# A one-element factor per softmax map and the sums of a head's norm: from GpSimd to VectorE

## The chip, the cores and the metric

The kernel runs on one core of a Trainium2 chip. A core has five engines, each with a queue of its own that it works through in order: TensorE (PE in the profile; PEld is its loading of weights), VectorE (DVE), ScalarE (ACT), GpSimd (POOL) and SyncE (SP), which here only issues DMAs. They wait for one another through semaphores. The metric is the device time of one execution in microseconds (us), lower being better; stated times are medians of several executions.

## What is computed

One encoder layer is applied to two groups of 1024 tokens with 1024 channels each. After a modulated RMS norm and one combined input projection there are two attention branches: A is grouped-query attention, B is differential attention with 4 heads, each with two 64-wide softmax maps. Both branch outputs are gated, projected, merged and projected once more. The change touches branch B only:

```python
def one(qblk):
    s = jnp.einsum('bqhmd,bkhmd->bhmqk', qblk, k).astype(jnp.float32) * scale
    p = jax.nn.softmax(s, axis=-1)
    pd = (p[:, :, 0] - lam * p[:, :, 1]).astype(v.dtype)
    return jnp.einsum('bhqk,bkhe->bqhe', pd, v)
...
ob = diff_attention(qb, kb, vb, lam)
ob = rms_norm(ob, subln_g) * (1.0 - lam_init)
```

## The kernel before

The two groups run one after the other through the same stages: projections for the first maps ("head"), six attention phases (0 and 1 for branch A, 2 to 5 for the four heads of branch B), and then the merge and output products. In the attention phases three streams of work are woven together: attention units, input projections of later heads (`qkb_gen`, `vb_gen`), and projections for the gates (`z_gen`). A scheduler decides the order on every engine from priorities and from its own estimate of when things are ready, so a small edit of the source can move many rows. A queue is then fixed: an instruction whose inputs aren't ready holds up everything behind it on its engine.

Matmuls work on pairs of halves (a value and its rest), which is why one product takes three matmuls. TensorE is given: 128x256 projections (L569), 128x512 gate projections (L755), scores (L789, L790, four matmuls a unit and map), values (L857 in branch A, L874 in branch B), transposes (L630, L961) and column sums (L885).

**A unit of branch B** covers one head and 256 queries, as two blocks of 128. For each block two softmax maps are made. `softmax_unit` (called in `scores`) issues the scores to PSUM, VectorE takes the negated row maximum (L791) and scales it (L792), ScalarE forms the exponentials and their sum (L793). The exponentials stay unnormalised: with sums su0 and su1, the difference of the two maps is formed as p0 + f·p1, where f = −lambda·su0/su1. So after the second map VectorE takes the reciprocal of su1 (L818), GpSimd multiplies it by su0 and by −lambda (L819), and in `flip` VectorE adds the maps with that factor (L833) and transposes the 32x32 blocks (L834). SyncE's queue then moves the result into place with four DMAs (L843), and TensorE multiplies by the values (L874, 8 matmuls a unit). There are 2 groups, 4 heads, 4 units a head, 2 blocks a unit: 64 factors.

**The norm of a head.** `b_values` squares the result (L878), sums the squares on TensorE (L885) and copies the sums to `ss` (L887). At the last of the four units (pr == 3) the head's norm is prepared: since the maps are unnormalised, the epsilon is weighted with su0 squared: su := su·su (L890), su := su·2·HD·EPS (L891), ss := ss + su (L892), ss := ss^(−1/2) (L893, a power, on GpSimd). These are [128, 8] tiles, 8 heads in all. The result is read only in `gated_gen` (L961), behind the attention phases.

**What else GpSimd does there.** For each 128-token tile of the next head's q and k: the power of its norm (L590), a product with it (L593), gains (L723) and the rotary steps (L615, L618 twice, L619), all on the tile `row`. L590 waits for two VectorE instructions, L588 and L589, which follow ScalarE's L584 and L585. `pairs_T` then has TensorE transpose `row` (L630). GpSimd also makes the low halves of weights (L195, L237). In the branch B phases `by_turns` gives all of the rotary work to GpSimd.

## Time and profile before

| | |
|---|---|
| median of 3 runs | 1890.05 us (1888.87 to 1896.09) |
| the profiled execution's own time | 1885.75 us |
| its span, first to last instruction | 1884.0 us |
| first factor of the first group, last of the second | at 468.7 us, at 1688.7 us |

The span's views speak of the profiled execution, whose own time is 4.30 us below the median of the runs and 1.75 us above its span. Busy time of PE counts overlapping matmuls once. A row of the groups names the line, the engine, the operation, the tile written and the tiles read, the shape and the count; behind the bar stand the busy time, the mean of one in ns, the idle time of the engine just ahead of these instructions, and who ended it. A row of the timeline has the start, the length, and in brackets the idle time ahead of it with its releaser.

### The profile page before, as it was taken

The numbers are of one execution on the slowest core, as the hardware profiler recorded it, in microseconds if no ns is written. First come the engines' busy times: TensorE is split into PE (matmuls) and PEld (weight loads), VectorE is DVE, ScalarE is ACT, GpSimd is POOL, SyncE is SP. The second block draws the span as 40 slices with busy tenths as digits, with TensorE's granted clock in tenths as the row PEclk, the third lists the DMA queues.
The fourth block names the chain that finished last, engine by engine and source line by source line (L and its number), as shares of the span: only waits on it lengthen the run. The fifth ranks groups of instructions, "written<-read, shape, count | busy, mean of one in ns | idle before, by whom it ended". The sixth has DMA issues, their size and how long they took to land.

```text
span 1884.0 us, 29900 instructions
## 1 busy us (share of the span) xinstructions
PE 1837.1 (98%) x10398; PEld 1552.8 (82%) x10398; DVE 1227.3 (65%) x2016; ACT 777.3 (41%) x1544; POOL 610.7 (32%) x888
## 2 busy tenths in 40 slices
PE   6999999999999999999999999999999999999999
PEld 3798878888899877888889887788888898888887
DVE  5777766454776777347466687665357856773795
ACT  4544434343554544213223444344344545442241
POOL 1343311442453452221233333014354635232100
PEclk7999999999999999999999999999999999999999
DMA  9135776564444467754631567666524443675442
GB/s 324 57 94 160 208 197 181 147 181 143 124 113 121 132 205 226 236 154 134 209 134 52 158 180 196 191 183 187 163 72 133 120 117 101 177 245 171 129 129 90
DMA packets 283895, 295.46 MB, mean 157 GB/s; under 512 B 41952, under 2 KB 236640, under 8 KB 283744
## 3 DMA queue, kind: packets, MB, share of 16 engines
q1 hardware_dynamic: 283744, 293.54, 53.1%
q8 instruction: 83, 1.36, 0.3%
q14 instruction: 68, 0.56, 0.1%
HBM read 133.98 MB, written 42.01 MB: 93 GB/s over the span
## 4 chain that ended last, share of the span: by engine, by line
PE 67%; issue 4%; DMA 4%; DVE 3%; POOL 3%; SPq 2%; ACT 1%; ACTq 0%; POOLq 0%; DVEq 0%
PE f L755 16%; PE f L569 14%; PE f L1029 7%; PE a L874 5%; PE s L789 4%; PE s L790 4%; PE a L857 3%; PE s L1029 3%; PE f L1064 3%; PE s L1064 2%; PE f L1136 2%; SPq L843 1%; PE s L1136 1%; DMA q<-p 1%; DMA st<-in_w_in_dram 1%
## 5 line engine op out<-in xcount | busy, mean ns | idle before, releaser
L755 PE MATMUL f<-u,w 128*128 128x512 f32 x2232 | 565.7, 396 | 1.0 <-POOL w L195 0.8
L755 PEld LDWEIGHTS f<-u,w 128*128 128x128 f32 x2232 | 410.5, 189 | 83.8 <-POOL w L195 1.8
L569 PE MATMUL f<-w,u 128*128 128x256 f32 x3456 | 472.7, 287 | 1.8 <-ACT row L584 0.6
L569 PEld LDWEIGHTS f<-w,u 128*128 128x128 f32 x3456 | 449.7, 192 | 23.2 <-issue 3.3
L791 DVE TENSOR_REDUCE m<-s 128x1 f32<-128x1024 f32 x256 | 309.4, 1217 | 104.4 <-PE s L790 102.4
L195 POOL TENSOR_TENSOR w<-st,w 128x512 fp32r<-128x512 f32 x160 | 214.1, 1356 | 394.5 <-ACT w L193 375.6
L834 DVE STREAM_TRANSPOSE p<-p 128x1024 f32<-128x1024 f32 x192 | 237.7, 1242 | 84.3 <-ACT p L793 68.2
L793 ACT ACTIVATE p<-s,m,u 128x1024 f32<-128x1024 f32 x128 | 153.9, 1204 | 164.8 <-issue 71.1
L790 PE MATMUL s<-u,sw 128*128 128x512 f32 x512 | 201.5, 398 | 0.0
L793 ACT ACTIVATE p<-s,m,rsB 128x1024 f32<-128x1024 f32 x128 | 153.8, 1203 | 107.2 <-DVE m L792 88.1
L193 ACT ACTIVATE w<-st 128x512 fp32r<-128x512 f32 x184 | 107.4, 626 | 99.5 <-DMA st<-in_w_in_dram 85.7
L1029 PE MATMUL f<-u,w 128*128 128x512 f32 x552 | 131.1, 392 | 0.0
L874 PE MATMUL a<-q,u 128*128 128x256 f32 x512 | 125.1, 381 | 2.8 <-DMA q<-p 1.9
L857 PE MATMUL a<-q,u 128*64 128x256 f32 x1024 | 117.9, 382 | 5.5 <-DMA q<-p 4.9
L1029 PEld LDWEIGHTS f<-u,w 128*128 128x128 f32 x552 | 103.0, 188 | 21.1
L590 POOL TENSOR_TENSOR rsB<-ss,nhalf 128x4 f32<-128x4 f32 x64 | 65.9, 1031 | 150.9 <-DVE ss L589 132.9
L633 DVE TENSOR_TENSOR u<-f,u 64x256 fp32r<-64x256 f32 (+1 forms) x198 | 81.4, 411 | 48.6 <-ACT u L632 43.3
L763 ACT ACTIVATE ev<-f 128x512 f32<-128x512 f32 x93 | 55.2, 594 | 139.0 <-PE f L755 90.3
L790 PEld LDWEIGHTS s<-u,sw 128*128 128x128 f32 x512 | 96.7, 189 | 16.8 <-issue 0.4
L789 PE MATMUL s<-u 128*128 128x512 f32 x256 | 107.6, 425 | 2.9 <-ACT p L793 2.9
L874 PEld LDWEIGHTS a<-q,u 128*128 128x128 f32 x512 | 94.7, 190 | 17.9 <-issue 3.3
L857 PEld LDWEIGHTS a<-q,u 128*64 128x64 f32 x1024 | 76.3, 137 | 40.0 <-issue 10.3
(221 smaller groups left out, 2181.6 us busy)
## 6 DMA issues: line engine op xcount, KB each, us to landing
q<-p SPq DMA_DIRECT2D x768, 128.0 KB, 2.6
st<-in_w_in_dram SPq DMA_DIRECT2D x132, 256.0 KB, 3.2
zd<-ev SPq DMA_DIRECT2D x96, 256.0 KB, 2.6
sw<-u SPq DMA_DIRECT2D x256, 64.0 KB, 2.0
u<-in_w_ada_dram SPq DMA_DIRECT2D x8, 1024.0 KB, 11.4
oo<-zd SPq DMA_DIRECT2D x64, 128.0 KB, 2.3
od<-oo SPq DMA_DIRECT2D x64, 128.0 KB, 2.4
st<-in_w_in_dram SPq DMA_DIRECT2D x64, 128.0 KB, 2.7
```

Of the source, the lines that this page charges most:

```text
L193: nc.scalar.activation(wh, st, AF.Copy)
L195: e.tensor_tensor(out=wl, in0=st, in1=wh.bitcast(F32), op=ALU.subtract)
L569: ins = nc.tensor.matmul(ps, lt[c][:, sl], w[:, c, wi, :], start=(k == 0), stop=(k == 23))
L755: ins = nc.tensor.matmul(ps, w[:, c, wi, e * P : (e + 1) * P], rt[c], start=(k == 0), stop=(k == 23),)
L789: nc.tensor.matmul(s[:, sl], q, k[:, sl], start=True, stop=False)
L790: nc.tensor.matmul(s[:, sl], sw, k[:, sl], start=False, stop=True)
L791: nc.vector.tensor_reduce(out=m, in_=s, axis=AX.X, op=ALU.max, negate=True)
L793: nc.scalar.activation(pt.rearrange("p (j c a) -> p j c a", j=4, c=8), s.rearrange("p (c a j) -> p j c a", c=8, j=4), AF.Exp, bias=m, scal ...
L834: nc.vector.transpose(pt, pt)
L857: lambda k=k, m=m: nc.tensor.matmul(acc[(LO, HI)[m]], u["v"][:, k], pT[m][:, k], start=(k == 0), stop=(k == 7))
L874: nc.tensor.matmul(acc, u["v"][:, k], pT[:, k], start=(k == 0), stop=(k == 7))
L1029: nc.tensor.matmul(ps, w[:, c, wi, d * P : (d + 1) * P], o[:, oi, :], start=(k == 0), stop=(k == 11))
```

## The change

The 64 factors are made by VectorE right behind the reciprocal. The two products on su become one VectorE instruction, and the addition to ss goes to VectorE too; the power stays on GpSimd. So 64 + 24 instructions leave GpSimd, and 64 + 16 are added to VectorE. The operations and their operands are otherwise the same.

```diff
@@ scores
             f = tiny.tile([P, 1], F32, tag="r", name=nm("r"))
             nc.vector.reciprocal(f, su)
-            nc.gpsimd.tensor_scalar(
+            nc.vector.tensor_scalar(
                 out=f, in0=f, scalar1=u["su"][:, qt : qt + 1], scalar2=nlam, op0=ALU.mult, op1=ALU.mult
             )
@@ b_values
             su = u["su"]
-            nc.gpsimd.tensor_tensor(out=su, in0=su, in1=su, op=ALU.mult)
-            nc.gpsimd.tensor_scalar(out=su, in0=su, scalar1=2.0 * HD * EPS, scalar2=1.0, op0=ALU.mult, op1=ALU.mult)
-            nc.gpsimd.tensor_tensor(out=ss, in0=ss, in1=su, op=ALU.add)
+            nc.vector.scalar_tensor_tensor(out=su, in0=su, scalar=2.0 * HD * EPS, in1=su, op0=ALU.mult, op1=ALU.mult)
+            nc.vector.tensor_tensor(out=ss, in0=ss, in1=su, op=ALU.add)
             nc.gpsimd.tensor_tensor(out=ss, in0=ss, in1=nhalf[:, :NTT], op=ALU.pow)
```

The scheduler rearranges the branch B phases of both groups: no matmul and no DMA is added or dropped, the rows up to the first factor of a group are the same, and from the end of branch B on they are the same again. In between PE's rows move by up to some 90 matmuls. The line of the power is L892 in the changed kernel; lines further down are one lower than before. Three places follow, all in the first group; first numbers in a tile's name count the tiles, and are the same in both kernels.

**First place: GpSimd, the last q and k tile of the fourth head** (`row_1109`; the fourth unit of the third head is near, whose norm is prepared here). Before:

```order
L590 TENSOR_TENSOR rsB_111<-ss_1110_7066,nhalf_97 128x4
L819 TENSOR_SCALAR r_1137_7195<-r_1137_7195,suB_2_119,nlam_116 128x1
L593 TENSOR_TENSOR row_1109_7063<-row_1109_7063,rsB_111 128x128
L890 TENSOR_TENSOR suB_2_119<-suB_2_119 128x8
L723 TENSOR_TENSOR row_1109_7063<-row_1109_7063,gB_114 128x2x48
L615 TENSOR_TENSOR rc_1111_7072<-row_1109_7063,tab_508_3287 128x4x16
L618 TENSOR_TENSOR row_1109_7063<-row_1109_7063,tab_508_3287 128x4x8 x2
L891 TENSOR_SCALAR suB_2_119<-suB_2_119 128x8
L619 TENSOR_TENSOR row_1109_7063<-rc_1111_7072,row_1109_7063 128x4x16
```

and with the change, on the same engine:

```order
L590 TENSOR_TENSOR rsB_111<-ss_1110_7064,nhalf_97 128x4
L593 TENSOR_TENSOR row_1109_7061<-row_1109_7061,rsB_111 128x128
L723 TENSOR_TENSOR row_1109_7061<-row_1109_7061,gB_114 128x2x48
L615 TENSOR_TENSOR rc_1111_7070<-row_1109_7061,tab_508_3287 128x4x16
L618 TENSOR_TENSOR row_1109_7061<-row_1109_7061,tab_508_3287 128x4x8 x2
L619 TENSOR_TENSOR row_1109_7061<-rc_1111_7070,row_1109_7061 128x4x16
```

The factor and the two products on su are gone from between the tile's rows. On PE the transpose of this row (L630) stands behind the same six matmuls in both kernels: four gate projections (L755) and the first two score matmuls of `s_1147`.

**Second place: GpSimd and VectorE, the first q and k tiles of the fourth head** (`row_1023`, `row_1032`, `row_1045`; `s_1057` and `s_1065` are scores of a unit of the third head). GpSimd before:

```order
L590 TENSOR_TENSOR rsB_111<-ss_1024_6542,nhalf_97 128x4
L590 TENSOR_TENSOR rsB_111<-ss_1033_6607,nhalf_97 128x4
L593 TENSOR_TENSOR row_1023_6539<-row_1023_6539,rsB_111 128x128
L590 TENSOR_TENSOR rsB_111<-ss_1046_6676,nhalf_97 128x4
L593 TENSOR_TENSOR row_1032_6604<-row_1032_6604,rsB_111 128x128
L723 TENSOR_TENSOR row_1023_6539<-row_1023_6539,gB_114 128x2x48
L615 TENSOR_TENSOR rc_1025_6548<-row_1023_6539,tab_508_3287 128x4x16
L618 TENSOR_TENSOR row_1023_6539<-row_1023_6539,tab_508_3287 128x4x8 x2
L593 TENSOR_TENSOR row_1045_6673<-row_1045_6673,rsB_111 128x128
L723 TENSOR_TENSOR row_1032_6604<-row_1032_6604,gB_114 128x2x48
L618 TENSOR_TENSOR row_1032_6604<-row_1032_6604,tab_508_3287 128x4x8 x2
L619 TENSOR_TENSOR row_1023_6539<-rc_1025_6548,row_1023_6539 128x4x16
```

GpSimd with the change:

```order
L590 TENSOR_TENSOR rsB_111<-ss_1024_6541,nhalf_97 128x4
L593 TENSOR_TENSOR row_1023_6538<-row_1023_6538,rsB_111 128x128
L723 TENSOR_TENSOR row_1023_6538<-row_1023_6538,gB_114 128x2x48
L615 TENSOR_TENSOR rc_1025_6547<-row_1023_6538,tab_508_3287 128x4x16
L618 TENSOR_TENSOR row_1023_6538<-row_1023_6538,tab_508_3287 128x4x8 x2
L619 TENSOR_TENSOR row_1023_6538<-rc_1025_6547,row_1023_6538 128x4x16
```

VectorE at the same place, before:

```order
L833 SCALAR_TENSOR_TENSOR p_1036_6630<-p_1040_6653,r_1044_6664,p_1036_6630 128x1024
L588 TENSOR_REDUCE ss_1024_6542<-row_1023_6539 128x4
L588 TENSOR_REDUCE ss_1033_6607<-row_1032_6604 128x4
L791 TENSOR_REDUCE m_1056_6728<-s_1057_6729 128x1
L834 STREAM_TRANSPOSE p_1036_6630<-p_1036_6630 128x1024
L589 TENSOR_SCALAR ss_1024_6542<-ss_1024_6542 128x4
L589 TENSOR_SCALAR ss_1033_6607<-ss_1033_6607 128x4
L791 TENSOR_REDUCE m_1064_6779<-s_1065_6780 128x1
```

and with the change:

```order
L833 SCALAR_TENSOR_TENSOR p_1036_6629<-p_1040_6652,r_1044_6663,p_1036_6629 128x1024
L834 STREAM_TRANSPOSE p_1036_6629<-p_1036_6629 128x1024
L791 TENSOR_REDUCE m_1056_6726<-s_1057_6727 128x1
L792 TENSOR_TENSOR m_1056_6726<-m_1056_6726,rsB_111 128x1
L791 TENSOR_REDUCE m_1064_6777<-s_1065_6778 128x1
L792 TENSOR_TENSOR m_1064_6777<-m_1064_6777,rsB_111 128x1
L588 TENSOR_REDUCE ss_1024_6541<-row_1023_6538 128x4
L589 TENSOR_SCALAR ss_1024_6541<-ss_1024_6541 128x4
```

GpSimd no longer mixes three tiles but finishes `row_1023` first, while VectorE now takes the sum of `row_1023` (`ss_1024`) behind the maximum of `s_1065`. On PE there stand, with the change, between the last score matmul of `s_1065` and the transpose of `row_1023`, 23 projection, 4 value and 8 score matmuls.

**Third place: VectorE and PE, the first values of a unit of the third head** (`a_1053`, which reads `q_1016`; its last block is `p_1020`, made from the scores `s_1030`). VectorE before:

```order
L818 RECIPROCAL r_1031_6587<-su_1028_6577 128x1
L879 TENSOR_TENSOR oo_1019_6521<-a_1018_6520,oo_1019_6521 128x4x2x32
L833 SCALAR_TENSOR_TENSOR p_1020_6523<-p_1027_6576,r_1031_6587,p_1020_6523 128x1024
L791 TENSOR_REDUCE m_1037_6631<-s_1038_6632 128x1
L834 STREAM_TRANSPOSE p_1020_6523<-p_1020_6523 128x1024
```

and with the change:

```order
L818 RECIPROCAL r_1031_6586<-su_1028_6576 128x1
L819 TENSOR_SCALAR r_1031_6586<-r_1031_6586,suB_2_119,nlam_116 128x1
L833 SCALAR_TENSOR_TENSOR p_1020_6522<-p_1027_6575,r_1031_6586,p_1020_6522 128x1024
L834 STREAM_TRANSPOSE p_1020_6522<-p_1020_6522 128x1024
```

PE before:

```order
L790 MATMUL s_1065_6780<-u_849_5428,sw_1017_6506 128x512
L569 MATMUL f_1035_6620<-w_1007_6462,u_77_328 128x256
L569 MATMUL f_1035_6620<-w_1007_6462,u_78_329 128x256
L874 MATMUL a_1053_6724<-q_1016_6501,u_939_6008 128x256 x8
L789 MATMUL s_1070_6822<-u_848_5427 128x512
```

and with the change:

```order
L569 MATMUL f_1035_6619<-w_1007_6461,u_70_276 128x256 x2
L874 MATMUL a_1053_6722<-q_1016_6500,u_939_6007 128x256 x2
L789 MATMUL s_1057_6727<-u_848_5427 128x512
L569 MATMUL f_1014_6484<-w_1007_6461,u_77_328 128x256
L569 MATMUL f_1014_6484<-w_1007_6461,u_78_329 128x256
L569 MATMUL f_1014_6484<-w_1007_6461,u_77_328 128x256 x2
```

On VectorE factor, addition and transposition now stand in a row. On PE the first value matmul has moved ahead of two maps' scores: between the last score matmul of `s_1030` and it stood 75 projection, 8 value, 16 score and 2 sum matmuls; now 55, 8, 8 and 2.

## Prediction

> **What bounds the kernel now.** I read the totals first, then the two stretches that the scheduler rearranges, then what TensorE waited for in them.
>
> ```profile
> PE 1837.1 (98%) x10398; PEld 1552.8 (82%) x10398; DVE 1227.3 (65%) x2016; ACT 777.3 (41%) x1544; POOL 610.7 (32%) x888
> ...
> 450.00:740.00 290.00, 285.82 (x1696) 249.34 (x1695) 203.93 (x344) 138.41 (x280) 129.60 (x239) 1.00 0.51 146
> 1385.00:1740.00 355.00, 349.31 (x1934) 304.55 (x1933) 237.14 (x380) 162.09 (x318) 151.32 (x245) 1.00 0.51 147
> ```
>
> The last two rows are the windows' view of branch B in each group (length, then busy time of PE, PEld, DVE, ACT, POOL, then the granted clock). PE is busy for 285.82 of 290 and 349.31 of 355 us, at full clock. Its matmuls stay the same, so if every idle moment of PE vanished from both stretches, the gain would be 4.18 + 5.69 = 9.87 us, 0.52% of 1890.05. VectorE is at 203.93 of 290 us (70%), so it has room. The largest of PE's waits in the same two stretches (total, times, longest):
>
> ```profile
> PE f L630 <- POOL row L619: 3.4, 2, 2.2
> PE a L874 <- DMA q<-p: 0.5, 1, 0.5
> ...
> PE f L630 <- POOL row L619: 1.5, 2, 1.2
> PE a L874 <- DMA q<-p: 1.4, 1, 1.4
> ...
> ```
>
> Only these two kinds have GpSimd's small work anywhere ahead of them: transposes that wait for a row of GpSimd (4.9 us), and values that wait for exponentials brought by DMA (1.9 us).
>
> **The busy time that changes engine.** These groups are what moves, and the nearest rows on VectorE.
>
> ```profile
> L819 POOL TENSOR_SCALAR r<-r,suB,nlam 128x1 f32<-128x1 f32 x64 | 22.8, 357 | 185.5 <-DVE r L818 168.6 <-DMA q<-p 9.1 <-DMA sw<-u 7.7
> L890 POOL TENSOR_TENSOR suB<-suB 128x8 f32<-128x8 f32 x8 | 8.9, 1117 | 0.4
> L891 POOL TENSOR_SCALAR suB<-suB 128x8 f32<-128x8 f32 x8 | 2.4, 303 | 0.7
> L892 POOL TENSOR_TENSOR ssB<-ssB,suB 128x8 f32<-128x8 f32 x8 | 1.6, 203 | 29.3 <-DVE ssB L887 22.3 <-DVE m L792 7.0
> L818 DVE RECIPROCAL r<-su 128x1 f32<-128x1 f32 x64 | 10.3, 160 | 52.4 <-ACT p L793 52.0
> L833 DVE SCALAR_TENSOR_TENSOR p<-p,r,p 128x1024 f32<-128x1024 f32 x64 | 87.8, 1372 | 25.6 <-POOL r L819 22.2 <-DMA sw<-u 1.6 <-DMA q<-p 1.1
> L589 DVE TENSOR_SCALAR ss<-ss 128x4 f32<-128x4 f32 x96 | 20.9, 219 | 1.4
> L792 DVE TENSOR_TENSOR m<-m,rsB 128x1 f32<-128x1 f32 x128 | 28.8, 231 | 1.8
> ```
>
> GpSimd loses 22.8 + 8.9 + 2.4 + 1.6 = 35.7 us of work, and its waiting for 64 reciprocals and 8 sums at the head of its queue. VectorE gains 64 factors and 16 instructions of the norm. The trace shows none of these forms on VectorE. From below, the reciprocal's 160 ns, since a small VectorE instruction of this kind is the cheapest here; from above, the 231 ns of the scaling; nothing lies under zero, as instructions are added to an engine. I take 219 ns, the nearest form (two scalars on few elements): 80 x 0.219 = 17.5 us, between 12.8 and 18.5. Against it stand the 22.2 us in 39 waits for GpSimd's factor ahead of L833 (0.57 us each), which go. So VectorE comes out about even, and the 17.5 us lie beside PE's work: were that cover gone in one stretch, half of it (8.7 us) less half the saved wait (11.1 us) would still be no loss. The factor waits for nothing that the reciprocal ahead of it hasn't waited for. The power on GpSimd now waits for VectorE's addition in place of the copy of the sums: 29.3 us for 8 now, with weight splits queued behind it, for which PE waits in neither list above; I put it at nothing, as that wait existed before.
>
> [...]
>
> **First place: GpSimd's queue under the transpose of `row_1109`.** The timeline shows PE's largest wait in either stretch:
>
> ```profile
> 679.98 1.02 POOL L590 TENSOR_TENSOR rsB<-ss,nhalf 128x4 f32<-128x4 f32 x1
> 680.99 0.34 POOL L819 TENSOR_SCALAR r<-r,suB,nlam 128x1 f32<-128x1 f32 x1
> 681.29 0.40 POOL L593 TENSOR_TENSOR row<-row,rsB 128x128 f32<-128x128 f32 x1
> 681.65 1.19 POOL L890 TENSOR_TENSOR suB<-suB 128x8 f32<-128x8 f32 x1
> 682.80 0.38 POOL L723 TENSOR_TENSOR row<-row,gB 128x96 f32<-128x96 f32 x1
> 683.97 0.20 POOL L891 TENSOR_SCALAR suB<-suB 128x8 f32<-128x8 f32 x1
> 684.25 0.32 POOL L619 TENSOR_TENSOR row<-rc,row 128x64 f32<-128x64 f32 x1
> 684.62 0.44 PE L630 MATMUL f<-ident,row 128*128 128x128 f32 x2 [2.18 <-POOL row L619]
> ```
>
> GpSimd runs without a gap, so each start minus the one before is the price: the factor 681.29 − 680.99 = 0.30, L890 682.80 − 681.65 = 1.15, L891 684.25 − 683.97 = 0.28, together 1.73 us. All three leave, and the rows on PE ahead of the transpose stay. The wait shrinks from 2.18 to 0.45: **−1.7 us** (at best −2.2, at worst 0 if the values behind it wait instead).
>
> **Second place: `row_1023`.**
>
> ```profile
> 638.95 0.42 ACT L585 ACTIVATE row<-row 128x256 f32<-128x256 f32 x1
> 639.72 2.00 POOL L590 TENSOR_TENSOR rsB<-ss,nhalf 128x4 f32<-128x4 f32 x2 [4.39 <-DVE ss L589]
> 640.84 0.41 DVE L588 TENSOR_REDUCE ss<-row 128x4 f32<-128x256 f32 x1
> 641.28 0.17 DVE L589 TENSOR_SCALAR ss<-ss 128x4 f32<-128x4 f32 x1
> 645.53 0.32 POOL L619 TENSOR_TENSOR row<-rc,row 128x64 f32<-128x64 f32 x1
> 645.90 0.33 PE L630 MATMUL f<-ident,row 128*128 128x128 f32 x1 [1.23 <-POOL row L619]
> ```
>
> Mixed with two other tiles, GpSimd took 645.85 − 639.72 = 6.1 us from the first power to the finished row. One tile by itself is L590, L593, L723, L615, L618 twice, L619: with the starts of the first place and no guests, 684.57 − 679.98 − 1.73 = 2.9 us. But its sum now stands behind the maximum of `s_1065`. From that map's last score: a maximum (1.2), its scaling (0.2), L588 (0.41), L589 (0.17), then 2.9, about 4.9 us with nothing else in the way. PE has 23 projection, 4 value and 8 score matmuls to do meanwhile, at the steps of these rows:
>
> ```profile
> 630.33 4.95 PE L569 MATMUL f<-w,u 128*128 128x256 f32 x40
> 638.91 3.69 PE L874 MATMUL a<-q,u 128*128 128x256 f32 x16 [0.47 <-DMA q<-p]
> 635.12 0.40 PE L789 MATMUL s<-u 128*128 128x512 f32 x1
> 635.35 0.40 PE L790 MATMUL s<-u,sw 128*128 128x512 f32 x1
> ```
>
> A projection is (635.12 − 630.33) / 40 = 0.12, a value about 3.69 / 16 = 0.23, a score 0.23: 2.8 + 0.9 + 1.8 = 5.5 us. So the row is ready 0.6 us early; a transposition of 1.23 us in VectorE's way would make it 0.6 late. The wait of 1.23 goes to between 0 and 0.6; I take **−1.0 us** (−1.2 to +0.5).
>
> **Third place: the values `a_1053`, where the new order costs.**
>
> ```profile
> 627.16 0.16 DVE L818 RECIPROCAL r<-su 128x1 f32<-128x1 f32 x1 [0.82 <-ACT p L793]
> 627.80 1.28 DVE L833 SCALAR_TENSOR_TENSOR p<-p,r,p 128x1024 f32<-128x1024 f32 x1
> 629.00 1.22 DVE L791 TENSOR_REDUCE m<-s 128x1 f32<-128x1024 f32 x1
> 630.14 1.23 DVE L834 STREAM_TRANSPOSE p<-p 128x1024 f32<-128x1024 f32 x1
> 632.40 3.39 SPq L843 DMA_DIRECT2D q<-p  x4
> ```
>
> The first value matmul (638.91 in the rows above) waits 0.47 us for these DMAs already. PE now has 20 projections and 8 scores less ahead of it: 2.4 + 1.8 = 4.2 us sooner. VectorE is sooner too: the factor follows the reciprocal (627.80 − 627.16 = 0.64 becomes about 0.16 + 0.22, −0.26), and the maximum between L833 and L834 is gone (630.14 − 629.00 = 1.14): 1.4 us. If the transfers then land as long after L834 as now (8.8 us), the wait becomes 0.47 + 4.2 − 1.4 = 3.3 us; if SyncE also issues them at once (they went out 1.0 us after L834's end, over 3.39 us), up to 2 us less, 1.3. So +0.8 to +2.8; I take **+1.5 us**, nearer the lower end, since the issues are what the order moves too.
>
> **The other waits.** The 1.4 us wait of values in the second group keeps its place within a few matmuls, and loses an average factor's wait: **−0.6 us** (−1.4 to 0). The row in the second group that PE waits 1.2 us for has no factor between its instructions: nothing. The DMAs on SyncE's queue (L843, `sw`, weights) are the same in number and move by a dozen places at most; the cost of that is in the third place's range.
>
> **Sum:** −1.7 − 1.0 + 1.5 − 0.6 = −1.8 us. The profiled execution, 1885.75 us (span 1884.0 and 1.75 around it), would become 1883.95. It lies 4.30 us below the median of the runs; on the runs' scale the forecast is 1890.05 − 1.8 = 1888.2 us, **no change that a measurement of this kernel can tell**, which is about 0.5% (9.5 us).
>
> **The rivals.**
>
> *Slower: PE arrives too early at the values.* The third place's mechanism, at more units. For it: the scheduler lets value matmuls start 2.4 + 1.8 us earlier there, by an estimate of VectorE and DMAs that this trace doesn't follow (8.8 us from L834 to the values). Against it: only one of the units is drawn forward so far. It decides once these waits add up to more than the 3.3 us gained elsewhere, i.e. two such places at 2.8. One in each of 8 heads: 8 x 2.8 − 3.3 = +19 us, 1909; in half of them +8, 1898. Chance 0.13, of which 0.09 lie beyond 0.5%.
>
> *Much faster: PE's busy time hides VectorE's wait.* The 22.2 us ahead of L833 lie on a chain through L834 and the DMAs to the values. If PE's matmuls were stretched by it rather than idle, all would come back: 1867.9 us. For it: PE's 98% is a modelled busy time. Against it: 40 projections in a row run at 0.12 us each with nothing to wait for, and PE waits for values only 1.9 us in both stretches. Chance 0.11. [...]
>
> *The change does nothing for PE.* GpSimd's rows wait for VectorE's sums (the 4.39 us ahead of L590 above), not for the factors, and the 1.7 us come back as a later wait of the values. Then the time is 1890 us within the runs' spread. Chance 0.20.
>
> *The forecast*, gains and one loss as summed, up to 6 us either way: 0.56.
>
> **How the numbers follow.** The range goes down to 1879.0, the limit of 9.87 us below 1890.05 and 1.2 for the spread of the runs (the lowest is 1888.87), and up to 1898, half the heads with a third place. Left out are the faster rival (0.11) and the far part of the slower one (0.08). Faster by over 0.5%: 0.11 and 0.01 of the forecast's edge, 0.12. Slower: 0.09. Within: 0.79.
>
> **What would show it.** Right: L819 as a VectorE group at 0.16 to 0.23 us with L833 no longer waiting for GpSimd; the wait at `row_1109` near 0.45 us; one wait of values of 1.3 to 3.3 us near 632 us; idle time of PE in both stretches within 3 us of 9.87. Wrong: PE's busy time in a stretch falling by more than 3 us with the same matmuls (the faster rival), or three or more waits of values over 1 us (the slower one).

## The result and the profile after

| | kernel before | changed kernel |
|---|---|---|
| median | 1890.16 us (20 runs, 1885.55 to 1896.44) | 1894.82 us (20 runs, 1891.70 to 1901.69) |
| ratio to before | | 1.0024, 95% interval 1.0015 to 1.0034 |
| the profiled execution's own time | 1885.75 us | 1893.75 us |

The change costs 4.7 us (a ratio of 1.0024) where 1.8 us were forecast as a gain. The totals, and the two windows of branch B with the same columns as before:

```profile
PE 1839.2 (97%) x10398; PEld 1552.2 (82%) x10398; DVE 1248.0 (66%) x2096; ACT 777.7 (41%) x1544; POOL 585.0 (31%) x800
```

```profile
450.00:740.00 290.00, 283.93 (x1684) 247.17 (x1683) 211.09 (x375) 137.50 (x278) 121.23 (x201) 1.00 0.51 145
1385.00:1740.00 355.00, 345.44 (x1909) 301.13 (x1908) 242.56 (x414) 159.11 (x316) 132.09 (x198) 1.00 0.49 143
```

The work moved as the diff says: VectorE has 20.7 us more, GpSimd 25.7 us less. (The moved rows alone were 35.7 us on GpSimd and are 22.6 us on VectorE. The other rows of GpSimd together take 10.0 us longer than before, those of VectorE 1.9 us less.) TensorE's busy time in the two windows fell because the windows hold 12 and 25 matmuls fewer; in the whole span it is 1839.2 us, 2.1 us more than before. So TensorE now stands idle for 290 − 283.93 = 6.07 and 355 − 345.44 = 9.56 us: 15.6 in place of 9.87. What it waited for (total, times, longest), the first group's stretch and then the second's:

```profile
PE s L789 <- DVE u L633: 1.4, 2, 1.2
PE f L755 <- DVE ssB L887: 1.3, 1, 1.3
PE f L630 <- POOL row L619: 1.2, 1, 1.2
PE a L874 <- DMA q<-p: 1.0, 1, 1.0
```

```profile
PE f L569 <- DVE u L633: 3.6, 1, 3.6
PE f L630 <- POOL row L619: 1.8, 2, 1.0
PE a L874 <- DMA q<-p: 1.7, 1, 1.7
PE f L569 <- DVE ssB L887: 1.3, 1, 1.3
```

The waits for GpSimd's rows fell in the first group from 3.4 to 1.2 us, and rose in the second from 1.5 to 1.8. A kind of wait is new: for VectorE to read a PSUM bank, L633 (the subtraction behind a transpose) or L887 (the copy of the sums). Before, this kind was 0.2 us in the two stretches together; now the rows of projections (L755, L569) that wait so add up to 1.3 + 3.6 + 1.3 = 6.2 us. The scores' 1.4 us (L789) name the same line but are of another kind: they wait for their operand, the tile `u` that L633 writes (see the first place, below).

The largest, 3.64 us, in the timeline of the changed kernel, VectorE's rows and then TensorE's (left out there are the other seven matmuls of the two score tiles):

```profile
1457.53 0.16 DVE L818 RECIPROCAL r<-su 128x1 f32<-128x1 f32 x1 [2.49 <-ACT p L793]
...
1459.35 0.42 DVE L633 TENSOR_TENSOR u<-f,u 64x256 fp32r<-64x256 f32 x1
1459.80 0.17 DVE L890 SCALAR_TENSOR_TENSOR suB<-suB 128x8 f32<-128x8 f32 x1
1459.89 0.41 DVE L588 TENSOR_REDUCE ss<-row 128x4 f32<-128x256 f32 x1
1460.21 1.22 DVE L791 TENSOR_REDUCE m<-s 128x1 f32<-128x1024 f32 x1
1461.35 0.41 DVE L588 TENSOR_REDUCE ss<-row 128x4 f32<-128x256 f32 x1
1461.67 1.24 DVE L834 STREAM_TRANSPOSE p<-p 128x1024 f32<-128x1024 f32 x1
1462.83 1.19 DVE L791 TENSOR_REDUCE m<-s 128x1 f32<-128x1024 f32 x1
1463.94 0.15 DVE L589 TENSOR_SCALAR ss<-ss 128x4 f32<-128x4 f32 x1
1464.12 0.43 DVE L633 TENSOR_TENSOR u<-f,u 64x256 fp32r<-64x256 f32 x1
```

```profile
1458.43 0.40 PE L789 MATMUL s<-u 128*128 128x512 f32 x1
...
1460.28 0.50 PE L885 MATMUL f<-ones_c,at 128*128 128x1 f32 x4
1460.64 0.42 PE L630 MATMUL f<-ident,row 128*128 128x128 f32 x2
1464.70 0.55 PE L569 MATMUL f<-w,u 128*128 128x256 f32 x1 [3.64 <-DVE u L633]
```

The pool of `f` has three banks (`ps_f`, bufs=3). By the rows, at 1461 us they hold a transpose of which VectorE has read one half (`f_2266`), the sums of L885 (`f_2273`) and a second transpose (`f_2279`), and the next projection needs one. VectorE works without a gap, but seven rows and 4.3 us lie between the two readings of `f_2266`. It had stood idle for 2.49 us just ahead, waiting for an exponential.

The same place in the kernel before, TensorE's rows and then VectorE's two readings of the transpose:

```profile
1456.13 1.35 PE L569 MATMUL f<-w,u 128*128 128x256 f32 x10
...
1458.25 0.50 PE L885 MATMUL f<-ones_c,at 128*128 128x1 f32 x4
1458.61 0.96 PE L569 MATMUL f<-w,u 128*128 128x256 f32 x6
1459.41 0.38 PE L630 MATMUL f<-ident,row 128*128 128x128 f32 x2
1460.10 3.01 PE L569 MATMUL f<-w,u 128*128 128x256 f32 x23 [0.31 <-ACT row L584]
```

```profile
1456.25 0.42 DVE L633 TENSOR_TENSOR u<-f,u 64x256 fp32r<-64x256 f32 x1
1458.50 0.43 DVE L633 TENSOR_TENSOR u<-f,u 64x256 fp32r<-64x256 f32 x1
```

There ten projections stand between the two score tiles and six between the sums and the transpose, and TensorE waits 0.31 us.

### The profile page after: what moved, and what is told of

The parts are those of the page before. It is cut to its first block, busy times and chain, and to the rows that moved or that the text cites. A ratio compares the mean times of both kernels' runs of the same rounds, so it can differ in the third digit from the quotient of the medians.

```text
span 1892.0 us, 29929 instructions
## 1 busy us (share of the span) xinstructions
PE 1839.2 (97%) x10398; PEld 1552.2 (82%) x10398; DVE 1248.0 (66%) x2096; ACT 777.7 (41%) x1544; POOL 585.0 (31%) x800
## 3 DMA queue, kind: packets, MB, share of 16 engines
q8 instruction: 83, 1.36, 0.3%
## 4 chain that ended last, share of the span: by engine, by line
PE 65%; DVE 7%; DMA 5%; issue 3%; SPq 2%; ACT 2%; POOL 2%; DVEq 0%; ACTq 0%; POOLq 0%
PE f L755 18%; PE f L569 14%; PE f L1028 7%; PE a L874 4%; PE a L857 4%; PE s L789 4%; PE s L790 4%; PE s L1028 3%; PE f L1135 2%; DVE m L791 2%; DMA q<-p 1%; DMA st<-in_w_in_dram 1%; ACT p L793 1%; PE s L1135 1%; SPq L843 1%
## 5 line engine op out<-in xcount | busy, mean ns | idle before, releaser
L755 PE MATMUL f<-u,w 128*128 128x512 f32 x2232 | 562.5, 395 | 1.8 <-DVE ssB L887 1.3
L569 PE MATMUL f<-w,u 128*128 128x256 f32 x3456 | 475.0, 287 | 7.2 <-DVE u L633 3.6
L755 PEld LDWEIGHTS f<-u,w 128*128 128x128 f32 x2232 | 409.7, 188 | 84.1 <-DVE ssB L887 1.3
L569 PEld LDWEIGHTS f<-w,u 128*128 128x128 f32 x3456 | 451.3, 192 | 28.8 <-issue 6.9
L791 DVE TENSOR_REDUCE m<-s 128x1 f32<-128x1024 f32 x256 | 309.1, 1217 | 102.1 <-PE s L790 100.5
L195 POOL TENSOR_TENSOR w<-st,w 128x512 fp32r<-128x512 f32 x160 | 218.2, 1382 | 506.0 <-ACT w L193 473.5
L834 DVE STREAM_TRANSPOSE p<-p 128x1024 f32<-128x1024 f32 x192 | 237.7, 1243 | 85.3 <-ACT p L793 66.6
L793 ACT ACTIVATE p<-s,m,u 128x1024 f32<-128x1024 f32 x128 | 153.9, 1204 | 165.8 <-issue 69.8
L793 ACT ACTIVATE p<-s,m,rsB 128x1024 f32<-128x1024 f32 x128 | 153.9, 1204 | 122.3 <-DVE m L792 96.5
L193 ACT ACTIVATE w<-st 128x512 fp32r<-128x512 f32 x184 | 108.0, 626 | 102.3 <-DMA st<-in_w_in_dram 86.2
L874 PE MATMUL a<-q,u 128*128 128x256 f32 x512 | 126.4, 380 | 3.1 <-DMA q<-p 2.7
L590 POOL TENSOR_TENSOR rsB<-ss,nhalf 128x4 f32<-128x4 f32 x64 | 67.0, 1048 | 185.3 <-DVE ss L589 165.3
L789 PE MATMUL s<-u 128*128 128x512 f32 x256 | 107.8, 426 | 3.2 <-ACT p L793 1.6
L633 DVE TENSOR_TENSOR u<-f,u 64x256 fp32r<-64x256 f32 (+1 forms) x198 | 81.4, 412 | 43.5 <-ACT u L632 38.2
L874 PEld LDWEIGHTS a<-q,u 128*128 128x128 f32 x512 | 94.7, 189 | 18.7 <-issue 3.7
```

What stands on the lines that cost most here:

```text
L193: nc.scalar.activation(wh, st, AF.Copy)
L195: e.tensor_tensor(out=wl, in0=st, in1=wh.bitcast(F32), op=ALU.subtract)
L569: ins = nc.tensor.matmul(ps, lt[c][:, sl], w[:, c, wi, :], start=(k == 0), stop=(k == 23))
L755: ins = nc.tensor.matmul(ps, w[:, c, wi, e * P : (e + 1) * P], rt[c], start=(k == 0), stop=(k == 23),)
L789: nc.tensor.matmul(s[:, sl], q, k[:, sl], start=True, stop=False)
L791: nc.vector.tensor_reduce(out=m, in_=s, axis=AX.X, op=ALU.max, negate=True)
```

## Where the 8 us between the two profiles lie

I number TensorE's matmuls in order of start (10398 in each kernel) and compare when the same number starts. The changed kernel's profiled run gains 0.3 us up to number 2800, loses 1.2 to 4400 (first group's branch B), loses 1.6 to 7200, gains 1.5 to 8000, **loses 5.3 from 8000 to 8480**, loses 1.7 to 9600, and nothing beyond: 8.0 us in sum. From 4450 to 7200 the two traces have the same rows, so these 1.6 us are of the run; the run of the kernel before that was profiled was also 4.4 us under its median. The other pieces lie where the orders differ and can be the change's own. By far the largest is the stretch from 8000 to 8480, about 1413 to 1503 us. Its window, before and after (same columns):

```profile
1412.46:1496.54 84.08, 82.07 (x481) 72.42 (x480) 67.21 (x115) 44.13 (x94) 47.60 (x91) 1.00 0.44 120
```

```profile
1413.47:1502.90 89.43, 82.80 (x481) 73.33 (x480) 69.47 (x125) 45.32 (x95) 44.29 (x80) 0.98 0.41 112
```

TensorE's idle time there goes from 2.01 to 6.63 us, and 3.3 us of the rise are at the place above. Its busy time is 0.73 us longer, at a granted clock of 0.98. This stretch is the measure in the experiments.

## The experiments

Two questions: is it the work on VectorE or the order? And what in the order? To keep them apart, a kernel is built twice: once to read off the row order that the scheduler gives, and once with that order written down for every engine, whatever engine the moved instructions are on:

```diff
+    for engine, line in hold(engines, rec["moved"]).items():
+        for a, b in zip(line, line[1:]):
+            tc.add_manual_dep(by_key[b], by_key[a].name, ...)
```

A moved instruction stands directly behind the VectorE instruction that feeds it. Where such work goes back to GpSimd (work_back_order_after, norm_order_none), GpSimd's own order is left to the scheduler; by the traces its other 800 instructions then stand in the held order but for 14 and 12 places. Lines cited from the edited kernels are 1 to 4 higher (L634 is L633, L794 is L793, L819 is the reciprocal's L818, L836 is L833, L877 is L874, L888 is L885, L890 is L887). All results, each ratio against the kernel before on the same chip; length and idle time are those of matmuls 8000 to 8480, read from windows like the two above:

| kernel | order, 1st / 2nd group | work on VectorE | ratio, 95% interval | length, idle (us) |
|---|---|---|---|---|
| changed kernel | after / after | all 80 | 1.0024, 1.0015–1.0034 | 89.43, 6.63 |
| work_moved_order_before | before / before | all 80 | 1.0008, 0.9994–1.0022 | 84.59, 2.40 |
| work_back_order_after | after / after | none | 1.0104, 1.0088–1.0120 | 91.02, 7.66 |
| factor_only | free | 64 | 1.0023, 1.0011–1.0035 | 89.61, 6.60 |
| second_group_after | before / after | all 80 | 1.0035, 1.0018–1.0051 | 90.38, 6.28 |
| second_group_before | after / before | all 80 | 1.0003, 0.9991–1.0016 | 86.16, 2.47 |
| before_again | before / before | none | 1.0012, 0.9997–1.0027 | 84.03, 1.99 |
| norm_only | free | 16 | 0.9984, 0.9974–0.9994 | 84.02, 2.00 |
| norm_order_none | as norm_only | none | 0.9998, 0.9987–1.0008 | 84.03, 2.01 |
| norm_order_all | as norm_only | all 80 | 1.0000, 0.9985–1.0014 | 84.58, 2.47 |
| rate_nudged | free, other rates | none | 0.9999, 0.9988–1.0011 | 84.03, 2.00 |
| mended_after | after, two rows moved | all 80 | 1.0023, 1.0012–1.0034 | 89.52, 5.89 |
| mended_more | after, four rows moved | all 80 | 1.0014, 1.0001–1.0027 | 89.98, 6.54 |
| scores_first | after, scores early | all 80 | 1.0021, 1.0009–1.0034 | 88.64, 6.83 |
| scores_first_mended | both | all 80 | 1.0004, 0.9991–1.0017 | 89.09, 5.59 |
| place_spread | after, the place as before | all 80 | 1.0004, 0.9994–1.0014 | 86.14, 4.22 |

### Work or order

**work_moved_order_before** and **work_back_order_after** swap the two.

> All 80 instructions are on VectorE as in the changed kernel, but every engine keeps the order of the kernel before; each moved instruction stands directly behind the VectorE instruction that feeds it (GpSimd's own order is left to the program). Theory O (the time lost comes from the new order of the instructions, the moved work costs nothing): the profiled run within 1883 to 1888 us, ratio to the kernel before 0.998 to 1.000, no TensorE wait of over 1 us for a PSUM read by VectorE (the subtraction L633, the copy of the sums) in the second group's maps. Theory W (VectorE's 20.7 us more of small instructions push back what stands behind them, wherever they stand): most of the 4.6 us, ratio 1.002 to 1.003, and TensorE idle 13 to 16 us in the two stretches of two-map attention.

> The factor and the preparations are on GpSimd as before, but the other instructions of all engines stand in the order of the changed kernel (GpSimd's own order is left to the program). Theory O: the loss stays, ratio 1.002 to 1.004, with the wait of about 3.6 us for L633 near 1461 us still there. Theory W: the loss goes, ratio 0.999 to 1.001. If the order of after is only good with the quick factor (39 waits for GpSimd of 0.3 to 0.8 us come back on VectorE, 22 us in all), the ratio is over 1.004: then order and work belong together.

With the order of before, the work on VectorE leaves the stretch nearly as it was (2.40 us idle). TensorE is idle for 11.0 us in the two windows, against 9.87 before and the 13 to 16 of theory W. That is nearer theory O, though not sharp: the ratio, 1.0008, and the profiled run, 1889.84 us, both lie above O's ranges, and the ratio's interval reaches from 0.9994 to 1.0022. With the order of after the wait near 1461 us is there even with the factor on GpSimd (3.7 us), so it is not the moved work's. But the third case came too: 1.0104. The order of after costs 15 us more if the factor is on GpSimd: VectorE's merge of the maps (L836) then waits 31.4 us for it, where L833 waited 22.2 us in the kernel before. So order and work belong together, and of these two orders it is only in that of after that the move is worth something. The groups of the reciprocal show how the orders differ, before, work_moved_order_before, after, work_back_order_after (behind the bar the idle time ahead of it, and the part that waited for the exponential):

```profile
L818 DVE RECIPROCAL r<-su 128x1 f32<-128x1 f32 x64 | 10.3, 160 | 52.4 <-ACT p L793 52.0
```

```profile
L819 DVE RECIPROCAL r<-su 128x1 f32<-128x1 f32 x64 | 10.3, 160 | 50.0 <-ACT p L794 49.5
```

```profile
L818 DVE RECIPROCAL r<-su 128x1 f32<-128x1 f32 x64 | 10.4, 162 | 73.2 <-ACT p L793 73.2
```

```profile
L819 DVE RECIPROCAL r<-su 128x1 f32<-128x1 f32 x64 | 10.4, 162 | 69.7 <-ACT p L794 69.6
```

In the order of after VectorE waits 17 to 21 us longer ahead of the reciprocal, whoever makes the factor. The 22.2 us of waits for GpSimd are gone (next rows, L833 of work_moved_order_before and of the changed kernel: 1.5 and 1.8 us idle in place of 25.6), but in the one order nothing comes of it, as TensorE had not been waiting for them, and in the other they are replaced.

```profile
L836 DVE SCALAR_TENSOR_TENSOR p<-p,r,p 128x1024 f32<-128x1024 f32 x64 | 84.6, 1323 | 1.5
```

```profile
L833 DVE SCALAR_TENSOR_TENSOR p<-p,r,p 128x1024 f32<-128x1024 f32 x64 | 85.8, 1340 | 1.8
```

**factor_only** (the first hunk of the change alone) and **norm_only** (the second alone), the scheduler free.

> Only the factor (64 of the 80 instructions, some 17 of the 20.7 us) is on VectorE, the preparations of the norm stay on GpSimd, and the scheduler is free: 836 of TensorE's rows stand otherwise than before, nearly as many as in the changed kernel (845). Theory O: the loss follows the order, which is nearly that of the changed kernel: ratio 1.001 to 1.004, with a wait of over 3 us near 1461 us. Theory W: 17 of 20.7 parts of the loss, ratio 1.001 to 1.003, with its idle time spread over many places.

> Only the preparations of the norm (16 of the 80 instructions, in place of 24 on GpSimd) are on VectorE, the factor stays on GpSimd, the scheduler is free: 188 of TensorE's rows stand otherwise than before, and the place near 1461 us should be as before. Theory P (the loss follows the order of the second group's place): matmuls 8000 to 8480 take 84 to 86 us, ratio 0.999 to 1.001. If the preparations on VectorE were what costs, ratio 1.002 to 1.003.

The factor alone brings the order of after, nearly row for row (the traces show another kind of matmul at 88 of TensorE's 10398 places), its 3.6 us wait and its loss. The preparations alone leave the stretch untouched, and the ratio, 0.9984, is under the 0.999 expected at least: the only one whose interval lies below 1. Is that a gain of the order or of the work?

> The order of norm_only with all the work on GpSimd as in the kernel before (GpSimd's own order is left to the program). If the gain of norm_only is one of the order: ratio 0.9975 to 0.9995. If it is one of the preparations made on VectorE: 0.9995 to 1.001.

> The order of norm_only (the fastest so far, ratio 0.9984) with all 80 instructions on VectorE, the factor's 64 directly behind their reciprocals. If the moved work is worth nothing either way and the order decides: ratio 0.9975 to 0.9995, as norm_only. If the factor on VectorE costs (some 17 us more of small instructions): 1.000 or more. If it gains, since 39 waits of VectorE for GpSimd go: under 0.9975.

It is not the order's: the same order gives 0.9998 with no moved work and 1.0000 with all of it, so the gain that was expected with the order did not come. By the letter of the two expectations the preparations then gain on VectorE and the factor costs as much. But the three intervals overlap, norm_only ran on another chip than the other two, and a kernel measured against itself is off by 0.12% (before_again, below). So 0.16% is not shown to be the work's either. In the two orders that keep the stretch whole, this one and that of before, the moved work as a whole is worth nothing that can be told.

**second_group_after** and **second_group_before** join the two orders between the groups, where they agree.

> All 80 instructions on VectorE; the first group in the order of the kernel before, the second group in the order of the changed kernel (the two orders are alike between, so they can be joined there). So far every run in the order of after lost 5.3 to 5.5 us of TensorE's time (6.9 with the work back on GpSimd) between its matmuls 8000 and 8480 (about 1413 to 1500 us), and the run in the order of before 0.5 us. Theory P (the loss is in that place): it is there again, 5 to 5.5 us, less some 1.3 us gained just ahead of it, so 3 to 4 us more than the moved work in the order of before: ratio 1.0015 to 1.003. Theory S (the loss is spread over all the maps, a little for each moved instruction or each reordered row): half of it, ratio 1.000 to 1.0015.

> The other way round: the first group in the order of the changed kernel, the second group in the order of the kernel before, all 80 instructions on VectorE. Theory P: matmuls 8000 to 8480 take 84 to 85 us as before and not 89.4, and the first group gives within 1.2 us of before: ratio 0.999 to 1.0008. Theory S: half of the loss, ratio 1.001 to 1.002, and as much as in the kernel joined the other way.

Theory P holds: the loss goes with the second group's order (1.0035 against 1.0003, intervals apart), and with 6.28 against 2.47 us idle. The first came out larger than the 1.003 expected at most; the second's 86.16 us are longer than the 85 expected at a granted clock of 0.98 in its window, with TensorE busy for 83.69 in place of 82.07 us.

**before_again** and **rate_nudged** ask how much of this any disturbance would do.

```diff
-    (1.229, 1.265, 0.9, 1.0, 0.85, 1.069),
+    (1.229, 1.265, 0.91, 1.01, 0.86, 1.079),
```

> The kernel before, with its own order written down for every engine: the same instructions in the same rows. A measure of what two profiles of one program differ by, and of whether writing the order down costs anything. Expected: ratio 0.9993 to 1.0007, matmuls 8000 to 8480 within 1 us of 84.1 us; the waits of the first profile that are an accident (and not of the order) differ by 1 to 3 us in single places.

> The kernel before, with nothing moved to VectorE, but four rates by which the second group's two-map attention is woven with other work raised by 0.01 (0.9 to 0.91, 1.0 to 1.01, 0.85 to 0.86, 1.069 to 1.079): 460 of TensorE's rows stand otherwise, about as many as the change moves in one group. Theory R (any such disturbance of the order moves the time by as much as the change did, since the order of before is a picked one): ratio 1.001 to 1.005, with a wait of over 1.5 us in the second group that the kernel before doesn't have. Against it: ratio 0.9993 to 1.0007.

The same program measured against itself gave 1.0012 with an interval up to 1.0027, wider than expected; so differences of 0.1% between kernels of this table mean nothing. Single waits differ too: one of values for a transfer, near 760 us where the rows of the three are the same, is absent in the profile of before, 1.36 us in before_again and 2.24 in rate_nudged. Theory R's loss did not come: 0.9999 with 460 other rows on TensorE. One wait of its kind did, 1.78 us of scores for an exponential at 1686 us (the kernel before waits 1.42 us for a transfer there). The nudge is a limited test, too: TensorE's rows differ in kind only between matmuls 8554 and 9505, so the stretch from 8000 to 8480 has its old pattern here, as it has in norm_only and its two followers. What the table does show is that the pattern goes with the loss: in all eight kernels with TensorE's rows of before in the stretch it is idle for 1.99 to 2.47 us, with none to all of the 80 instructions on VectorE, and in the eight that keep after's run of rows near 1461 us, mended ones included, for 5.59 to 7.66 us.

### What in the order

**mended_after** moves two VectorE rows up at the place of the 3.64 us, in the order of after:

```diff
   L588 ss_2264
+  L633 f_2266, second half
   L791 m_2260
+  L887 f_2273
   L588 ss_2277
   L834 p_2235
   L791 m_2270
   L589 ss_2264
-  L633 f_2266, second half
-  L887 f_2273
```

> The changed kernel in its own order with two VectorE rows moved up at one place, near 1460 us: the second subtraction of tile f_2266 stands three reads of PSUM and row sums earlier (behind the first row sum instead of behind two maxima and a transposition), and the copy of the sums f_2273 directly behind the first maximum. Theory O: the wait of 3.64 us on TensorE goes, 0 to 0.6 us are left of it, and the time falls by 3 to 3.6 us against the changed kernel: ratio to the kernel before 1.0003 to 1.001. Theory W: VectorE is late there by all that stands in its queue, so the wait comes back within the next 10 us, for the next subtraction or the next probabilities: ratio 1.002 to 1.003.

**mended_more** moves two more: L792 of `m_2260` directly behind its L791, and the first L633 of `f_2279` ahead of L834.

> As the first mended kernel, in whose profile the wait of 3.64 us was gone but came back 24 matmuls later as a wait of 3.09 us of the scores for the exponential. Here what that exponential waits for is moved up as well: the small product behind the first maximum stands directly behind it (before: behind a transposition, a second maximum and a subtraction), and the next subtraction of tile f_2279 stands ahead of the transposition, so that ScalarE's queue, which waits for it, comes free. Theory Q (only the order of VectorE's queue is at fault; its work fits): both waits go, matmuls 8000 to 8480 take 85 to 86.5 us and not 89.4, and the ratio is 0.9995 to 1.0012. Theory W (VectorE has too much to do in that stretch): 2.5 us or more of the wait turn up once more within 15 us, ratio 1.0018 to 1.003.

What TensorE waited for from 1450 to 1475 us in mended_after, and in mended_more:

```profile
PE s L790 <- ACT p L794: 3.1, 1, 3.1
```

```profile
PE a L877 <- DMA q<-p: 3.0, 1, 3.0
PE s L790 <- ACT p L794: 0.8, 1, 0.8
```

The wait for the bank is gone both times, and one of 3 us takes its place 24 to 28 matmuls on: first the scores wait for an exponential whose maximum was late, then, with that put right, the values wait for the transposed map that L834 now makes later. Theory W came true as to the waits and the stretch; mended_more's ratio, 1.0014, lies between the ranges of the two theories. But W's reason, that VectorE is too full, was still open, since it idles 2.1 and 2.5 us just ahead. **scores_first** goes for that idle time: the score tiles `s_2237` and `s_2241`, woven into eight value matmuls, come whole ahead of them.

```diff
+  L789, L790 s_2237 and s_2241, 8 matmuls in a row
   L874 a_2233, 8 matmuls
-  (L789, L790 of both woven in between, and four behind)
```

> The changed kernel in its own order but for one place, 10 us ahead of the wait at 1461 us: TensorE computes the two score tiles s_2237 and s_2241 whole ahead of the values a_2233, with which they were interleaved (eight rows moved), VectorE takes their maxima at once and multiplies the output of the values after the merge of the maps, and ScalarE takes the two exponentials ahead of the square of the values. VectorE had stood idle there for 2.09 and 2.49 us, for the values and for the second exponential, with the reads of PSUM queued behind. Theory Q (the place is late because of the order, from TensorE's scores on, and VectorE has time enough): the reciprocal at 1457.5 us comes 2.2 to 3.3 us earlier, the wait of 3.64 us shrinks to under 1.2 us and does not come back, matmuls 8000 to 8480 take 85 to 87 us and not 89.4, ratio 1.000 to 1.0012. Theory W (VectorE has too much in that stretch, whatever its order): a wait of 2.5 us or more within 20 us behind, ratio 1.0018 to 1.003.

> The place of scores_first and the first mended place together (the second subtraction of f_2266 and the copy of f_2273 moved up in VectorE's queue). Theory Q: none of the waits for PSUM reads, exponentials or transfers between matmuls 8273 and 8301 is over 0.6 us, matmuls 8000 to 8480 take 84.5 to 86 us, ratio 0.9995 to 1.001. Theory W: 2.5 us or more still waited there, ratio 1.0018 to 1.003.

The reciprocal comes at 1451.97 us, 5.6 earlier (of which 2.2 were this run's lead at matmul 8000), but VectorE then waits 2.23 us for the next scores, and TensorE still 3.0 us for L633. Both together: 2.8 us for the exponential again. scores_first_mended's ratio, 1.0004, doesn't fit its profile, which has the loss (89.09 us); its interval reaches to 1.0017, and I leave it open.

So none of the four orders tried for VectorE's queue takes the wait away while TensorE's run of rows stays. That run differs most from before: in the order of after two score tiles, the sums and a transpose follow one another in 14 matmuls, 8 + 4 + 2, with nothing between them. In the order of before ten and six projections stand between. **place_spread** puts TensorE's rows so, on top of scores_first, and the rows of VectorE and ScalarE there in the pattern of before:

```diff
   L630 f_2266
   L569 f_2267, 12 matmuls
+  L789, L790 s_2261
+  L569 f_2267, 6 matmuls
-  L569 f_2267, 12 matmuls
-  L789, L790 s_2261
   L789, L790 s_2271
   L885 f_2273
+  L569 f_2267, 6 matmuls
   L630 f_2279
```

> The changed kernel in its own order, but with the whole place near 1461 us laid out as in the kernel before: the scores ahead of the values as in scores_first, and in place of two score tiles, the sums and the transposition in one run of TensorE's rows, eight matmuls of the projection stand between the two score tiles and six between the sums and the transposition; VectorE's and ScalarE's rows there follow the pattern of before (25 rows differ on TensorE, 14 on VectorE, 8 on ScalarE). Theory D (the loss is that of a pile: what VectorE and ScalarE must answer comes in one run of TensorE's rows, and three banks hold for less time than the answers take): matmuls 8000 to 8480 take 84.5 to 86.5 us and not 89.4, no wait of over 1.3 us between matmuls 8260 and 8310, ratio 0.9995 to 1.0012. Theory W (VectorE, 20.7 us fuller, cannot follow in that stretch whatever the order): a wait of 2.5 us or more, matmuls 8000 to 8480 88 us or more, ratio 1.0015 to 1.003.

Built, it has six projections between the score tiles and not the eight that the text names. The place in place_spread, TensorE and then VectorE:

```profile
1456.12 0.40 PE L790 MATMUL s<-u 128*128 128x512 f32 x1
...
1457.05 0.87 PE L570 MATMUL f<-w,u 128*128 128x256 f32 x6
...
1458.68 0.50 PE L888 MATMUL f<-ones_c,at 128*128 128x1 f32 x4
1459.05 0.96 PE L570 MATMUL f<-w,u 128*128 128x256 f32 x6
1459.85 0.38 PE L631 MATMUL f<-ident,row 128*128 128x128 f32 x2
1460.54 3.13 PE L570 MATMUL f<-w,u 128*128 128x256 f32 x24 [0.32 <-ACT row L585]
```

```profile
1456.66 0.42 DVE L634 TENSOR_TENSOR u<-f,u 64x256 fp32r<-64x256 f32 x1
...
1458.85 0.43 DVE L634 TENSOR_TENSOR u<-f,u 64x256 fp32r<-64x256 f32 x1
```

The wait is 0.32 us in place of 3.64, none took its place within the next 80 matmuls, and the two readings of a transpose start 2.2 us apart in place of 4.8. The stretch takes 86.14 us, 3.3 less than in the changed kernel: 2.4 us of idle time and 0.9 us of busy time, at a granted clock of 1.00 in place of 0.98. The ratio is 1.0004, with an interval that ends just below the changed kernel's. Since scores_first_mended has the same ratio with the loss in its profile, the stretch is the clearer sign, and it rests on one profile. All 80 instructions are still on VectorE, so theory W falls and D stands for the large wait. What is left of the stretch's loss (4.22 us idle against 2.01) lies in four waits of 0.9 to 1.2 us. Three of them, at 1432, 1479 and 1498 us, stand at the same matmuls in the changed kernel; the fourth, 0.89 us for ScalarE's L585 at 1475 us, does not. Their causes are open. TensorE's run of rows was not spread without the changes to the two queues, so what spreading does alone isn't shown; the four kernels with changed queues and the run kept waited 2.8 to 3.8 us there.

## The prediction, step by step

**It was wrong, and the step that failed is the closing of the sum.** It took four terms (−1.7 − 1.0 + 1.5 − 0.6) from waits that the profile of before has, with the sentence "Only these two kinds have GpSimd's small work anywhere ahead of them", and so put every other wait of the new order at nothing. The changed kernel has 6.2 us of a kind that the old one has 0.2 us of: PSUM banks held until VectorE reads them. The largest, 3.64 us, goes with the new order and lies in the second group, from which no place was read. The order of the rows there could have been read for it: two score tiles, the sums and a transpose on TensorE without a projection between them. That the 1894.82 us still lie below the 1898 of the range's upper end is luck: that room was made for waits of the values, which did not come.

**The moved work beside TensorE's**: right in what it costs there, by the held orders. Its size was off: the 80 instructions take 22.6 us in place of 17.5, over the upper bound of 18.5. The changed kernel's groups:

```profile
L819 DVE TENSOR_SCALAR r<-r,suB,nlam 128x1 f32<-128x1 f32 x64 | 17.4, 273 | 2.1
L890 DVE SCALAR_TENSOR_TENSOR suB<-suB 128x8 f32<-128x8 f32 x8 | 2.8, 348 | 0.0
L891 DVE TENSOR_TENSOR ssB<-ssB,suB 128x8 f32<-128x8 f32 x8 | 2.4, 304 | 0.2
```

The prediction took the nearest row, L589 with a mean of 219 ns (its median is 170), for a form with two scalars. It has one, a constant of the code; L819 reads two from tiles, and takes 273 ns. That this is the reason wasn't tried. The medians of L890 and L891 are 164 and 166 ns, near the 160 ns of the lower bound; their means are about twice that, as four of the 16 took longer (last section).

**The 22.2 us of waits ahead of L833** went, as said. That they would balance VectorE's account was right for the order of before and wrong for the order of after, where VectorE waits 20.8 us more ahead of the reciprocal.

**First place**: right in kind, the size too large. The wait went from 2.18 to 1.24 us, not to 0.45. In the old order, with the work moved, it is 0.91 us, so the work alone is worth 1.3 of the 1.7 us. In the new order factor and products are gone from between the rows, but the weight splits ahead of the row's power (L195, 3.8 us in both) start 1.44 us later, at 677.63 in place of 676.19 us, since the order moved the tile ahead of them. And 1.16 us of a new wait for L633 follow 4 us behind.

```profile
684.78 0.44 PE L630 MATMUL f<-ident,row 128*128 128x128 f32 x2 [1.24 <-POOL row L619]
...
688.77 0.50 PE L789 MATMUL s<-u 128*128 128x512 f32 x1 [1.16 <-DVE u L633]
```

These scores need the transposed row. VectorE was free for it, but ScalarE's half of the work, L632, stood behind a weight split (L193) that waited for its weights:

```profile
687.23 0.63 ACT L193 ACTIVATE w<-st 128x512 fp32r<-128x512 f32 x1 [1.04 <-DMA st<-in_w_in_dram]
688.30 0.42 DVE L633 TENSOR_TENSOR u<-f,u 64x256 fp32r<-64x256 f32 x1 [2.93 <-ACT u L632]
```

A wait at this matmul is in all ten kernels with all 80 instructions on VectorE, in either order, with 0.3 to 1.5 us (1.50 in work_moved_order_before), and in none of the seven others. So what the sum took as a gain came back in part or in whole: TensorE came sooner and met the next wait. The third rival had that, though with the values as the ones to wait.

**Second place**: right, and narrowly. TensorE's wait for `row_1023`, 1.23 us, is gone (−1.0 was forecast). GpSimd took 4.1 us for the tile (642.02 to 646.12) and not 2.9, as L723 took 1.43 us there, and the row was ready just as TensorE came to it. The gain is the order's: with the order of before and the work moved the wait is 1.23 us as before. **Third place**: wrong. No wait came, and the old 0.47 us went; the value matmuls stand woven between projections and scores and find their data there. **Other waits**: the values' wait in the second group is 1.7 in place of 1.4 us, not 0.6 less.

**The rivals.** The slower one, TensorE too early at the values, did not come: the waits for transfers of values are 1.0 and 1.7 us. The time was lost in another way. The much faster one falls: the 22.2 us left the chain and no time with them. "The change does nothing for PE" comes closest to what the held orders show of the work alone. Of what was to show the forecast right only one thing came, that L833 no longer waits for GpSimd.

## What to carry to other kernels

Where a scheduler makes the order, a moved instruction has two prices, its own and that of the order it brings (here ratios of 1.0008 in the old order and 1.0024 in the new); write the old order down and run the moved work in it to get them apart. Read the new order for runs of rows on the busiest engine whose results all need the same other engine, against the number of banks that hold them. Here mending the answering queue only handed the wait on (3.1 and 3.0 us in place of 3.64); spreading the run, with the two answering queues laid out to match, took it away (0.32 us). Waits on an engine that the end of the program isn't waiting for can vanish and give nothing: 39 waits of VectorE for GpSimd's factor, 22.2 us, went, and in the order of before the ratio was 1.0008.

## What the runs showed of the hardware that was not expected

In the changed kernel two VectorE instructions of 128x8 took over 1 us, an L890 1.25 us and an L891 1.29. When GpSimd was idle, L890 took 0.15 to 0.17 us. The L890 of 1.25 us, and GpSimd at the time:

```profile
1540.32 1.25 DVE L890 SCALAR_TENSOR_TENSOR suB<-suB 128x8 f32<-128x8 f32 x1
```

```profile
1539.45 3.36 POOL L195 TENSOR_TENSOR w<-st,w 128x512 fp32r<-128x512 f32 x2 [29.26 <-ACT w L193]
```

The row of GpSimd is two splits; the first lasts 2.10 us and ends at 1541.55, and L890 ends at 1541.57. Of the 16 instructions L890 and L891 four took over 0.2 us; in each case a TENSOR_TENSOR of GpSimd on a whole row or weight was under way and ended within 0.03 us of it. Beside a power (L590) L891 took 0.17 us. The 64 factors, one tensor and two scalars, took 265 to 276 ns throughout, also the four that started under a split L195. In the profile of before, 13 of VectorE's products L792, which read two tiles as L890 and L891 do, started under an L590 and took 0.15 to 0.17 us; 30 that started under a split L195 had a median of 0.69 us, and none of them ended before the split did. Why these instructions end with a split and not with a power isn't shown.
